# Opening of the first FFN in blocks of 128 channels: scale and shift as single columns on TensorE, squares of x summed there

## The chip, the cores and the metric

The kernel runs on one core of a Trainium2 chip. The metric is device time in microseconds (us), lower is better. The engines of the core are TensorE (PE; PEld is its weight load), VectorE (DVE), ScalarE (ACT), GpSimd (POOL) and SyncE (SP, which issues most of the DMAs).

## The reference, cut to what matters

One encoder layer, 1024 tokens of 1024 channels in f32: an FFN, a mixer of two attentions, and a second FFN, each behind a modulated norm. Scale and shift of every norm come from a conditioning vector through one wide matrix. The change touches only the first norm.

```python
def rms_norm(x, g):
    y = xf * lax.rsqrt(jnp.mean(xf * xf, axis=-1, keepdims=True) + NORM_EPS)
    return (y * g).astype(x.dtype)

def modulate(x, g, shift, scale):
    return rms_norm(x, g) * (1 + scale[:, None, :]) + shift[:, None, :]

cond = jax.nn.silu(c)
mod = (cond @ ada_w[l] + ada_b[l]).reshape(B, N_SUBLAYERS, 3, D_MODEL)
h = modulate(x, norm_g[l, 0], mod[:, 0, 0], mod[:, 0, 1])
x = x + 0.5 * mod[:, 0, 2][:, None, :] * swiglu(h, ffn1_w1[l], ffn1_w3[l], ffn1_w2[l])
```

## The kernel before

Channels lie on the 128 partitions and tokens along the free dimension, so x is eight blocks of 128 channels by two halves of 512 tokens. A scale or a shift of a block is then one column of 128 values. Index i = 0 of the modulation is the shift and i = 1 the scale; each needs the product of `cond` (1024 values, held as eight columns) with a slice of `ada_w`.

A matrix product splits both operands into a rounded f32r part and a rest (`wh`, `wl` and the two tiles named `h`) and takes three f32r matmuls (`mm3`). The first half of the FFN is done in pairs of output blocks (`UpPair`, eleven pairs of fourteen steps) by a scheme with seven products (Strassen's), and the second half in `Down`. A step of a pair is `product`: four channel blocks of three matmuls each, into one PSUM bank. There are eight banks of 512 f32: four tagged "y", for the first products of pairs 0 and 1, and four tagged "b" for everything else. The first two steps of pairs 0 to 3 need only channel blocks 0 to 3 and tokens 0 to 511. They can't start before the norm of these tokens and scale and shift of these blocks are known. That is the opening.

The whole stage up to the end of the first FFN is written down as a list of tasks (class `Plan`) and put in an order by a list scheduler at build time (`flush`, lines 478 to 519): it tries some fifty settings with its own table of durations and keeps the order with the earliest end. Each engine then runs its own queue in that order. Between `nc.inorder = True` and `False` (lines 363 to 386) the DMAs on SP's queue keep the order in which they are written; everything else is free to move as far as data and buffers let it.

The opening as it is written (lines 363 to 395):

- `load_x` brings eight tiles of x, 256 KB each.
- `SquareSum.add` (line 569) squares each tile on ScalarE, and VectorE adds it to a sum `nacc`. Four f32 matmuls of zeros by x warm TensorE up.
- `ModQuarter.load` (line 1546) brings scale and shift weights of 256 channels: per quarter and per index four tiles of 256 KB, whose row pieces are 1 KB. The order on SP's queue is quarter 0, the weights of pairs 0 and 1, quarter 1, those of pairs 2 and 3.
- `norm_rms` sums `nacc` over the partitions by four matmuls with a column of ones, `norm_root` takes the root in twelve small operations of VectorE, and `norm_spread` lays it over all partitions, in one bank.
- For the scale, `ModQuarter.add` (line 1554) accumulates eight weight pieces on VectorE (`macc`) and turns the sum into columns with two matmuls by ones. For the shift, `ModQuarter.row` (line 1565) runs eight matmuls with `cond` as the weight, which give a row of 256 values on one partition (`mrow`), and turns that into columns.
- `mod_done` (line 1594) adds the bias and, for the scale, forms A = (1 + scale) * g.
- `Operands.block` (line 1638) scales the tile of x by A and the root on VectorE, adds the shift on ScalarE while rounding (`h`), and forms the rest on VectorE.
- `run(i)` issues the first two steps of pair i.

Later in the same stage scale and shift of channels 512 to 1023 follow (`ModHalf`), then x blocks 4 to 7 and the other half of the tokens. `t512` takes its tiles from a pool of 52.

Of the kernel before, what the change touches and what calls it, by code (L numbers as in the profile page):

```python
# [11 lines left out]
F32 = mybir.dt.float32  # L12
# [5 lines left out]
AF = mybir.ActivationFunctionType  # L18
ALU = mybir.AluOpType
# [4 lines left out]
D = 1024  # L24
# [3 lines left out]
H = 512  # L28
# [29 lines left out]
class View:  # L58


    def __init__(self, tile, ops):
        self.tile, self.ops = tile, ops
# [500 lines left out]
class SquareSum:  # L563
# [5 lines left out]
    def add(self, x):  # L569
        nc = self.k.nc  # L570
        sq = t512(self.k, name="nsq" if self.acc else "nacc")
        nc.scalar.activation(sq, x, AF.Square)
        if self.acc:
            self.eng.tensor_add(self.acc, self.acc, sq)
        else:
            self.acc = sq
        return sq


def norm_rms(k, acc, tmp, ptile):  # L580

    nc = k.nc
    ps = ptile()
    for b in range(4):
        nc.tensor.matmul(ps[:, b:b + 1], acc[:, b * 128:b * 128 + 128], k.ones_col, start=True, stop=True)
    return norm_root(k, ps[:, 0:4], tmp)


def norm_root(k, t, tmp):

    v = tmp.tile([128, 4], F32, tag="nv", name="nv", bufs=1)
    k.nc.vector.tensor_scalar(v, t, 1.0 / D, EPS, op0=ALU.mult, op1=ALU.add)
    r = tmp.tile([128, 4], F32, tag="nr", name="nr", bufs=1)
    rsqrt(k, r, v, tmp, "na", 1)
    return r
# [132 lines left out]
def t512(k, dt=F32, name="t", home="c"):  # L728

    p, tag, n = k.homes[home]  # L730
    return p.tile([128, H], dt, tag=tag, name=name, bufs=n)
# [748 lines left out]
class ModHalf:  # L1480
# [6 lines left out]
    def load(self, upto):  # L1487
        k = self.k
        for kc in range(len(self.raws), min(8, upto)):
            t = self.tile("mraw")  # L1490
            k.nc.sync.dma_start(t, k.ada_w[kc * 128:kc * 128 + 128, self.i * D + self.h * H:self.i * D + self.h * H + H])
            self.raws.append(t)
# [12 lines left out]
    def columns(self):  # L1505

        t = self.bank()
        for b in range(4):
            self.k.nc.tensor.matmul(t[:, b:b + 1], self.acc[:, b * 128:b * 128 + 128], self.k.ones_col, start=True, stop=True)
        mod_done(self.k, self.i, t, 4 * self.h, 4)  # L1510
# [24 lines left out]
        mod_done(k, self.i, cols, 4 * self.h, 4)  # L1535


class ModQuarter:


    N = 256

    def __init__(self, k, i, q, bank):
        self.k, self.i, self.q, self.bank, self.raws = k, i, q, bank, []

    def load(self, g):
        k, n = self.k, self.N
        t = t512(k, name="mraw")
        c0 = self.i * D + self.q * n
        k.nc.sync.dma_start(t.rearrange("p (a n) -> p a n", a=2),  # L1550
                            k.ada_w[g * 256:g * 256 + 256, c0:c0 + n].rearrange("(a p) n -> p a n", p=128))
        self.raws += [t[:, 0:n], t[:, n:2 * n]]

    def add(self):
        k, nc = self.k, self.k.nc
        acc = t512(k, name="macc")[:, 0:self.N]
        for kc, t in enumerate(self.raws):
            c = k.cond[:, kc:kc + 1]
            if kc == 0:
                nc.vector.tensor_scalar(acc, t, c, None, op0=ALU.mult)  # L1560
            else:
                nc.vector.scalar_tensor_tensor(acc, t, c, acc, op0=ALU.mult, op1=ALU.add)
        self.done(acc, k.ones_col)

    def row(self):
        k, nc = self.k, self.k.nc
        t = self.bank()[0:1, 0:self.N]
        for kc, r in enumerate(self.raws):
            nc.tensor.matmul(t, k.cond[:, kc:kc + 1], r, start=kc == 0, stop=kc == 7)
        r = t512(k, name="mrow")[0:1, 0:self.N]  # L1570
        nc.scalar.activation(r, t, AF.Copy)
        self.done(r, k.ones_col[0:1, :])

    def done(self, v, one):
        t = self.bank()
        for b in range(2):
            self.k.nc.tensor.matmul(t[:, b:b + 1], v[:, b * 128:b * 128 + 128], one, start=True, stop=True)
        mod_done(self.k, self.i, t, 2 * self.q, 2)


def side_by_side(gens):
# [12 lines left out]
def mod_done(k, i, t, b0, n):  # L1594
    nc = k.nc
    m = k.mod[:, i * 8 + b0:i * 8 + b0 + n]
    nc.vector.tensor_add(m, t[:, 0:n], k.ada_b[:, i * 8 + b0:i * 8 + b0 + n])
    s, j = i // 3, i % 3
    c8 = slice(s * 8 + b0, s * 8 + b0 + n)
    if j == 1:  # L1600
        nc.vector.scalar_tensor_tensor(k.A[:, c8], m, 1.0, k.ng[:, c8], op0=ALU.add, op1=ALU.mult)
    elif j == 2:
        nc.vector.tensor_scalar(k.G[:, c8], m, 0.5, None, op0=ALU.mult)
# [619 lines left out]
def layer(tc, xT, c, pos, ada_w, ada_b, ng, inv, w13a, w2a, w_a, w_f, w_q, w_g, fb, fg, dg, wbr, wout, w13b, w2b, out):  # L2223
    with ExitStack() as es:
        k = K()
# [63 lines left out]
        with ExitStack() as ph:  # L2289
            k.wq = wq = Halves(k, pool(w0s, "w0", True, side="right"), 6, [nc.vector, nc.gpsimd])  # L2290
            rp = k.c
# [3 lines left out]
            bank = lambda: pp.tile([128, H], F32, tag="b", name="b", bufs=4)  # L2295
            nc.on = True
            z = t512(k, F32R, "zr")
            nc.gpsimd.memset(z.bitcast(F32), 0.0)
            seed_banks(k, pp, z)
            x = [[t512(k, name="x") for _ in range(2)] for _ in range(8)]  # L2300
            rms = [None, None]
# [5 lines left out]
            pairs = [UpPair(k, i, w13a, wq, bank, d_g[0], nc.vector) for i in range(PAIRS)]  # L2307
# [3 lines left out]
                q.first = True  # L2311
            ops = Operands(k, 0, x, nc.vector)
            mod = {i: ModHalf(k, i, 1, bank) for i in range(2)}
            quarter = [[ModQuarter(k, i, q, bank) for i in range(2)] for q in range(2)]
            k.up_step, k.stores = 0, []

            def consts():
# [46 lines left out]
            for i in range(8):  # L2364
# [2 lines left out]
            nc.gpsimd.memset(on, 1.0)  # L2367
            nc.gpsimd.affine_select(k.ident, on, pattern=[[-1, 128]], compare_op=ALU.is_equal, fill=0.0, base=0,
                                    channel_multiplier=1)
            sq = SquareSum(k, nc.vector)  # L2370
            warm = bank()
            for i in range(8):
                t = sq.add(x[i][0])
                if i < 4:
                    nc.tensor.matmul(warm, z.bitcast(F32)[:, 0:128], x[i][0], start=True, stop=True)
            for n in range(4):
                for m in quarter[0]:
                    m.load(n)
            for i in range(2):
                pairs[i].load1("c", (0,))  # L2380
            for n in range(4):
                for m in quarter[1]:
                    m.load(n)
            for i in range(2, 4):
                pairs[i].load1("c", (0,))
            nc.inorder = False
            rms[0] = norm_rms(k, sq.acc, rp, bank)
            ops.rb[0] = norm_spread(k, rms[0], bank)
            for m in quarter:
                m[1].add()  # L2390
                m[0].row()
            for c in range(4):
                ops.block(c)
            for i in range(4):
                run(i)
# [15 lines left out]
            sq = SquareSum(k, nc.vector)  # L2411
# [63 lines left out]
            ps = [bank() for _ in range(4)]  # L2475
# [100 lines left out]
        bank = lambda: pp.tile([128, H], F32, tag="b", name="b", bufs=4)  # L2576
        with ExitStack() as ph:
# [10 lines left out]
            rp = pool(ph, "rms", True, side="right")  # L2588
# [9 lines left out]
            m = branches(k, w_b, bank, {c: [mods(6)] for c in range(1, 4)})  # L2598
            x = [[t512(k, name="xb") for _ in range(2)] for _ in range(8)]
# [118 lines left out]
```

## Time and profile before

| | us |
|---|---|
| median of 3 runs | 2113.43 |
| lowest and highest run | 2113.41, 2115.27 |
| span of the profiled execution | 2110.5 |

The span runs from the first to the last recorded instruction of the one profiled execution; the page gives no other time of that execution. A run's time is some 3 us longer than the span. A row of the timeline gives start, length, engine, source line, operation, output and inputs by their names in the program, shapes and count; consecutive rows of one kind are merged. All instructions of the planned stage have line L198, that of the scheduler's helper, so they are told apart by tile names. An f32 matmul in the source stands in the trace as two weight loads and two matmuls, an f32r matmul as one of each. Matmuls overlap, so the distance between starts, not the length of one, tells what an instruction costs.

Busy time in the first stretches, in us:

| stretch | PE | DVE | ACT | DMA, GB/s |
|---|---|---|---|---|
| 8 to 10 | 1.79 | 1.69 | 1.87 | 353 |
| 14 to 16 | 1.53 | 1.90 | 0.00 | 359 |
| 18 to 20 | 1.31 | 1.88 | 1.34 | 353 |
| 22 to 24 | 2.00 | 1.97 | 0.00 | 350 |

### The profile page before, as it was taken

The page shows a single profiled execution, that of the slowest core. Times are in us where ns is not written, and L with a number is a line of the kernel's source. Part 1 is how long each engine was busy: PE and PEld are TensorE (multiplying, and loading weights), DVE is VectorE, ACT ScalarE, POOL GpSimd, SP SyncE. Part 2 cuts the span into 40 slices and gives each one's busy share as a digit, 9 for nine tenths or more (in the row PEclk, how much of TensorE's full clock was granted, in tenths as well). Part 3 has the DMA queues.
Part 4 walks back from the last instruction along what each step waited for, and adds up shares of the span by engine and source line. Part 5 has one row for each costly group of instructions (what it writes and reads, how often), then busy time and mean ns, then how long its engine had stood idle before and what let it go on. Part 6 is the DMA issues. An engine that isn't in the chain of part 4 may idle for free.

```text
span 2110.5 us, 30999 instructions
## 1 busy us (share of the span) xinstructions
PE 2094.6 (99%) x10296; PEld 1728.2 (82%) x10296; DVE 1641.7 (78%) x3167; ACT 1135.6 (54%) x2075; POOL 251.1 (12%) x397
## 2 busy tenths in 40 slices
PE   8999999999999999999999999999999999999999
PEld 5887888888888888888888888888888888888887
DVE  7989887869977399886998877979975765568554
ACT  5754444445456266688776776335543333334443
POOL 0022222321100000000444332000000000000000
PEclk9999999999999999999999999999999999999999
DMA  9468888899721555668543224794142523375511
GB/s 347 134 215 275 303 295 274 277 379 366 261 92 48 172 174 192 217 244 274 192 158 99 86 66 160 252 315 154 46 130 100 194 85 129 101 264 206 189 50 41
DMA packets 218285, 398.72 MB, mean 189 GB/s; under 512 B 27198, under 2 KB 69694, under 8 KB 217100
## 3 DMA queue, kind: packets, MB, share of 16 engines
q1 hardware_dynamic: 199772, 339.24, 48.0%
q0 software_dynamic: 18064, 57.46, 7.1%
q8 instruction: 81, 1.33, 0.3%
q14 instruction: 80, 0.66, 0.1%
q10 hardware_dynamic: 288, 0.05, 0.0%
HBM read 282.62 MB, written 114.03 MB: 188 GB/s over the span
## 4 chain that ended last, share of the span: by engine, by line
PE 91%; issue 3%; DVE 2%; DMA 2%; ACT 1%; POOL 1%; SPq 0%; POOLq 0%; DVEq 0%; ACTq 0%
PE b L198 37%; PE y L198 28%; PE pj L198 12%; PE py L198 7%; PE p L198 4%; PE pt L198 4%; DMA mraw<-in_ada_w 0%; POOL d_g L198 0%; DMA f<-d_f 0%; DMA wr<-in_w13b 0%; ACT nt L198 0%; DMA d_wf10l<-pre 0%; DVE z L198 0%; DMA x<-in_xT 0%; ACT h L198 0%
## 5 line engine op out<-in xcount | busy, mean ns | idle before, releaser
L198 PE MATMUL b<-h,wh 128*128 128x512 f32 x1408 | 436.5, 390 | 0.5 <-DVE z L198 0.4
L198 PE MATMUL y<-h,wh 128*128 128x512 f32 x1280 | 397.1, 390 | 0.4 <-ACT h L198 0.3
L198 ACT ACTIVATE wh<-wr 128x512 fp32r<-128x512 f32 x308 | 192.6, 629 | 316.0 <-PE b L198 166.1
L198 PEld LDWEIGHTS b<-h,wh 128*128 128x128 f32 x1408 | 263.2, 188 | 59.1 <-DVE z L198 3.4
L198 PEld LDWEIGHTS y<-h,wh 128*128 128x128 f32 x1280 | 239.6, 188 | 53.4 <-issue 1.2
L198 DVE TENSOR_TENSOR wl<-wr,wh 128x512 fp32r<-128x512 f32 x308 | 208.4, 686 | 94.4 <-ACT wh L198 88.8
L198 PE MATMUL b<-h,wl 128*128 128x512 f32 x704 | 273.6, 389 | 0.0
L198 PE MATMUL y<-h,wl 128*128 128x512 f32 x640 | 249.0, 389 | 0.0
L198 PE MATMUL pj<-wh,h 128*128 128x512 f32 x512 | 161.3, 391 | 0.0
L198 PEld LDWEIGHTS b<-h,wl 128*128 128x128 f32 x704 | 132.2, 188 | 27.7
L198 PEld LDWEIGHTS y<-h,wl 128*128 128x128 f32 x640 | 120.1, 188 | 24.8
L198 ACT ACTIVATE wh<-g 128x512 fp32r<-128x512 f32 x154 | 96.0, 624 | 80.2 <-PE b L198 55.7
L198 PE MATMUL b<-wh 128*128 128x512 f32 x352 | 137.0, 389 | 0.7 <-ACT mrow L198 0.7
L198 DVE TENSOR_TENSOR wl<-a,wh 128x512 fp32r<-128x512 f32 x132 | 90.8, 688 | 59.9 <-ACT wh L198 55.7
L198 PE MATMUL b<-wl,wh 128*128 128x512 f32 x352 | 136.9, 389 | 0.0
L198 PE MATMUL b<-wh,wl 128*128 128x512 f32 x352 | 136.8, 389 | 0.0
L198 ACT ACTIVATE wh<-a 128x512 fp32r<-128x512 f32 x132 | 82.4, 625 | 99.9 <-PE b L198 60.3
L198 DVE TENSOR_TENSOR wl<-g,wh 128x512 fp32r<-128x512 f32 x154 | 105.6, 686 | 29.6 <-ACT wh L198 29.1
L198 POOL TENSOR_SCALAR pr<-pr,mn 128x128 f32<-128x128 f32 (+7 forms) x128 | 102.3, 816 | 167.3 <-DVE mn L198 135.1
L198 ACT ACTIVATE pth<-pt 128x512 fp32r<-128x512 f32 (+1 forms) x160 | 85.5, 554 | 55.9 <-PE pt L198 54.3
L198 DVE TENSOR_TENSOR ptl<-pt,pth 128x512 fp32r<-128x512 f32 (+1 forms) x160 | 97.9, 632 | 20.1 <-ACT pth L198 18.6
L198 PEld LDWEIGHTS pj<-wh,h 128*128 128x128 f32 x512 | 95.7, 188 | 18.6
(382 smaller groups left out, 4376.4 us busy)
## 6 DMA issues: line engine op xcount, KB each, us to landing
g<-d_g SPq DMA_DIRECT2D x154, 256.0 KB, 5.3
mraw<-in_ada_w SPq DMA_DIRECT2D x144, 256.0 KB, 5.7
wr<-in_w13a SPq DMA_DIRECT2D x112, 256.0 KB, 5.4
wr<-in_w13b SPq DMA_DIRECT2D x88, 256.0 KB, 4.8
d_g<-z POOLq DMA_DIRECT2D x77, 256.0 KB, 5.8
d_g<-z SPq DMA_DIRECT2D x77, 256.0 KB, 3.2
a<-in_w2a SPq DMA_DIRECT2D x44, 256.0 KB, 6.3
a<-in_w2b SPq DMA_DIRECT2D x44, 256.0 KB, 5.3
```

The source lines that it names most:

```text
L198: getattr(getattr(self.tc.nc, engine), op)(*map(real, a), **{n: real(v) for n, v in kw.items()})
```

## The change

Scale and shift of the first four channel blocks are no longer made in quarters of 256 channels, but block by block. A block loads its weights as two tiles per index (row pieces of 512 B) and forms its two columns directly: the weight piece is the stationary operand, one column of `cond` the moving one, eight matmuls accumulate a column, the scale's first. VectorE's sums and the shift's rows go. The squares of x stay on ScalarE, but each squared tile is summed over the partitions by four matmuls with the column of ones, and all eight tiles accumulate in four columns of one bank; `nacc` and its additions go. Four matmuls of zeros, which clear that bank, take the place of the warm-up on x. The DMAs on SP's queue are now block 0, pair 0, block 1, pairs 1 and 2, block 2, pair 3, block 3. The columns of a block are written down ahead of that block's operands.

```diff
@@ -1535,47 +1535,33 @@
         mod_done(k, self.i, cols, 4 * self.h, 4)
 
 
-class ModQuarter:
-
-
-    N = 256
-
-    def __init__(self, k, i, q, bank):
-        self.k, self.i, self.q, self.bank, self.raws = k, i, q, bank, []
-
-    def load(self, g):
-        k, n = self.k, self.N
-        t = t512(k, name="mraw")
-        c0 = self.i * D + self.q * n
-        k.nc.sync.dma_start(t.rearrange("p (a n) -> p a n", a=2),
-                            k.ada_w[g * 256:g * 256 + 256, c0:c0 + n].rearrange("(a p) n -> p a n", p=128))
-        self.raws += [t[:, 0:n], t[:, n:2 * n]]
-
-    def add(self):
-        k, nc = self.k, self.k.nc
-        acc = t512(k, name="macc")[:, 0:self.N]
-        for kc, t in enumerate(self.raws):
-            c = k.cond[:, kc:kc + 1]
-            if kc == 0:
-                nc.vector.tensor_scalar(acc, t, c, None, op0=ALU.mult)
-            else:
-                nc.vector.scalar_tensor_tensor(acc, t, c, acc, op0=ALU.mult, op1=ALU.add)
-        self.done(acc, k.ones_col)
-
-    def row(self):
-        k, nc = self.k, self.k.nc
-        t = self.bank()[0:1, 0:self.N]
-        for kc, r in enumerate(self.raws):
-            nc.tensor.matmul(t, k.cond[:, kc:kc + 1], r, start=kc == 0, stop=kc == 7)
-        r = t512(k, name="mrow")[0:1, 0:self.N]
-        nc.scalar.activation(r, t, AF.Copy)
-        self.done(r, k.ones_col[0:1, :])
-
-    def done(self, v, one):
+class ModBlock:
+
+
+    def __init__(self, k, c, bank):
+        self.k, self.c, self.bank = k, c, bank
+
+    def load(self):
+
+        k, c = self.k, self.c
+        self.raws = {}
+        for i in (1, 0):
+            for j in range(2):
+                t = t512(k, name="mraw")
+                c0 = i * D + c * 128
+                k.nc.sync.dma_start(t.rearrange("p (a n) -> p a n", a=4),
+                                    k.ada_w[j * H:j * H + H, c0:c0 + 128].rearrange("(a p) n -> p a n", p=128))
+                self.raws[i, j] = t
+
+    def columns(self):
+
+        k, nc, c = self.k, self.k.nc, self.c
         t = self.bank()
-        for b in range(2):
-            self.k.nc.tensor.matmul(t[:, b:b + 1], v[:, b * 128:b * 128 + 128], one, start=True, stop=True)
-        mod_done(self.k, self.i, t, 2 * self.q, 2)
+        for i in (1, 0):
+            for kc in range(8):
+                w = self.raws[i, kc // 4][:, kc % 4 * 128:kc % 4 * 128 + 128]
+                nc.tensor.matmul(t[:, i:i + 1], w, k.cond[:, kc:kc + 1], start=kc == 0, stop=kc == 7)
+            mod_done(k, i, t[:, i:i + 1], c, 1)
 
 
 def side_by_side(gens):
@@ -2311,7 +2297,7 @@
                 q.first = True
             ops = Operands(k, 0, x, nc.vector)
             mod = {i: ModHalf(k, i, 1, bank) for i in range(2)}
-            quarter = [[ModQuarter(k, i, q, bank) for i in range(2)] for q in range(2)]
+            blocks = [ModBlock(k, c, bank) for c in range(4)]
             k.up_step, k.stores = 0, []
 
             def consts():
@@ -2367,29 +2353,24 @@
             nc.gpsimd.memset(on, 1.0)
             nc.gpsimd.affine_select(k.ident, on, pattern=[[-1, 128]], compare_op=ALU.is_equal, fill=0.0, base=0,
                                     channel_multiplier=1)
-            sq = SquareSum(k, nc.vector)
-            warm = bank()
+            ps = bank()
+            for _ in range(4):
+                nc.tensor.matmul(ps, z[:, 0:128], z, start=True, stop=True)
             for i in range(8):
-                t = sq.add(x[i][0])
-                if i < 4:
-                    nc.tensor.matmul(warm, z.bitcast(F32)[:, 0:128], x[i][0], start=True, stop=True)
-            for n in range(4):
-                for m in quarter[0]:
-                    m.load(n)
-            for i in range(2):
-                pairs[i].load1("c", (0,))
-            for n in range(4):
-                for m in quarter[1]:
-                    m.load(n)
-            for i in range(2, 4):
-                pairs[i].load1("c", (0,))
+                t = t512(k, name="nsq")
+                nc.scalar.activation(t, x[i][0], AF.Square)
+                for b in range(4):
+                    nc.tensor.matmul(ps[:, b:b + 1], t[:, b * 128:b * 128 + 128], k.ones_col, start=False, stop=i == 7,
+                                     skip_group_check=True)
+            for c in range(4):
+                blocks[c].load()
+                for i in ((0,), (1, 2), (3,), ())[c]:
+                    pairs[i].load1("c", (0,))
             nc.inorder = False
-            rms[0] = norm_rms(k, sq.acc, rp, bank)
+            rms[0] = norm_root(k, ps[:, 0:4], rp)
             ops.rb[0] = norm_spread(k, rms[0], bank)
-            for m in quarter:
-                m[1].add()
-                m[0].row()
             for c in range(4):
+                blocks[c].columns()
                 ops.block(c)
             for i in range(4):
                 run(i)
```

## The prediction

> **What bounds the kernel now.** I read the page first, for the bounding engine.
>
> ```profile
> span 2110.5 us, 30999 instructions
> PE 2094.6 (99%) x10296; PEld 1728.2 (82%) x10296; DVE 1641.7 (78%) x3167; ACT 1135.6 (54%) x2075; POOL 251.1 (12%) x397
> ```
>
> TensorE is busy for 99% of the span. A saved instruction on another engine is worth something only where TensorE waits for it. So the second view is the chain of waits at the start (start, length, what), which is the stage that changes.
>
> ```profile
> 4.09 5.21 DMA x<-in_xT
> 9.32 6.03 DMA mraw<-in_ada_w
> ...
> 19.34 0.76 DVE x L198
> 20.12 0.73 ACT h L198
> 20.89 0.73 PE y L198 x2
> 21.63 0.95 PE b L198 x4
> 22.58 1.36 PE y L198 x5
> 23.94 0.95 PE b L198 x4
> 24.89 1.35 PE y L198 x5
> 26.24 0.95 PE b L198 x4
> 27.20 0.89 PE y L198 x3
> 28.09 0.53 PE b L198 x4
> 28.62 0.66 PE y L198 x2
> 29.28 0.34 PE b L198 x4
> 29.62 1.74 PE y L198 x7
> ...
> 387.25 5.44 PE y L198 x24
> ```
>
> Up to 20.89 the first product waits for x (landed at 9.30), the scale and shift weights (15.35), and then a serial tail of TensorE and VectorE. From 20.89 on every row is TensorE. The "y" rows are the first products; the "b" rows between them are the scale and shift of channels 256 to 511, with 3 x 0.95 + 0.53 + 0.34 = 3.7 us. The last row gives the price of a product instruction in a steady stream: 5.44 / 24 = 0.227 us. The third view, TensorE's waits from 30 to 720 us, asks whether anything later can still be won.
>
> ```profile
> PE b L198 <- ACT mrow L198: 0.7, 1, 0.7
> PE b L198 <- DVE z L198: 0.4, 1, 0.4
> ```
>
> Two more are 0.2 each, 1.5 us in all. After 20.89 the opening is bound by the number of TensorE instructions. So I compare one number: **the time of the first product plus all TensorE work behind it that isn't a product**. Before, that is 20.9 + 3.7 = 24.6 us (work common to both kernels, from 33 us on, left out).
>
> **The change part by part.**
>
> ```profile
> 47.53 1.84 PE L198 MATMUL b<-ones_col,macc 128*128 128x1 f32 x16
> 49.23 0.72 PE L198 MATMUL b<-h,wh 128*128 128x512 f32 x2
> ...
> 62.56 1.05 PE L198 MATMUL b<-ident,nr 128*128 128x128 f32 x8
> 63.37 0.71 PE L198 MATMUL y<-h,wh 128*128 128x512 f32 x2
> ```
>
> *Price of a single column.* Eight source matmuls of a full-width weight by one column stand as 16 instructions, so each f32 matmul is two. They start at 47.53, and the next product starts at 49.23: 1.70 / 16 = 0.106 us an instruction. The spread of the root-mean-square is 8 instructions in 63.37 - 62.56 = 0.81 us.
>
> *Removed.* Two quarters of the shift as rows (16 instructions of 0.95 / 4 = 0.24 us each), their turn into columns, the four matmuls that end the sum of squares, four f32 warm-up matmuls on x, and on VectorE the sums below.
>
> ```profile
> L198 DVE SCALAR_TENSOR_TENSOR macc<-mraw,cond,macc 128x256 f32<-128x256 f32 x14 | 6.7, 482 | 0.2
> L198 DVE TENSOR_TENSOR nacc<-nacc,nsq 128x512 f32<-128x512 f32 x7 | 4.8, 692 | 4.9 <-ACT nsq L198 4.4
> ```
>
> VectorE sheds 6.7 + 4.8 us and two 0.35 us starts. Four more additions and two more products on the modulation columns come to it, about 1 us by the 0.15 of the nv row below. From 30 us on TensorE waited 0.4 us for VectorE in all, so of that relief only what lies ahead of the first product counts.
>
> *Squares on TensorE.* Eight tiles x 4 matmuls x 2 = 64 instructions, 6.8 us at 0.106, 0.85 us a tile.
>
> ```profile
> 4.49 0.63 ACT L198 ACTIVATE nacc<-x 128x512 f32<-128x512 f32 x1 [1.26 <-DMA x<-in_xT]
> ...
> 6.66 4.04 ACT L198 ACTIVATE nsq<-x 128x512 f32<-128x512 f32 x6 [0.90 <-DMA x<-in_xT]
> ```
>
> ScalarE delivers the first squares at 5.1, the third at 7.3, and from there one every 0.67 us to 10.70. TensorE needs 0.85 for each, so it falls behind from the third on: 7.3 + 6 x 0.85 = 12.4 us. That holds at full clock. The clock was not full from the start:
>
> ```profile
> 7.23 0.34 PEld L198 LDWEIGHTS b<-x,zr 128*128 128x128 f32 x1 [0.52 <-issue]
> 7.91 0.19 PEld L198 LDWEIGHTS b<-x,zr 128*128 128x128 f32 x1 [0.34 <-issue]
> ```
>
> A weight load took 0.34 until 7.23 and 0.19 from 7.91. That is 0.15 more, which makes a slow single column about 0.26, an estimate from these two rows. If the clock rises at 7.5 again, nine instructions are done by then and 55 x 0.106 = 5.8 follow: 13.3 us. The squares end at **12.4 to 13.3**.
>
> *The root.* Twelve VectorE operations, for the second half at 59.58 to 61.91 (two rows, first and last):
>
> ```profile
> 59.58 0.15 DVE L198 TENSOR_SCALAR nv<-b 128x4 f32<-128x4 f32 x1
> 61.74 0.17 DVE L198 SCALAR_TENSOR_TENSOR nr<-na,nr 128x4 f32<-128x4 f32 x1
> ```
>
> These are 2.3 us on a free VectorE, so the root is there at 14.7 to 15.6. TensorE meanwhile does block 0.
>
> *Columns.* Each block is 2 x 8 x 2 = 32 instructions, 3.4 us: 13.6 us for four blocks, where rows and their turns took 3.8 + 0.5 + 0.3 a quarter, 9.3 in all. Block 0 follows the squares (12.4 to 15.8, or 13.3 to 16.7), and with the spread of 0.8 TensorE reaches 16.6 or 17.5. Scaling and h then take the 0.76 + 0.73 of the chain, and the first product starts at 18.1 to 19.0, some 2.4 us sooner than now. Meanwhile TensorE runs block 1's columns.
>
> *DMA.* The bytes and their place on SP's queue are nearly the same: 16 tiles of modulation weights and 8 of products, now as 4, 2, 4, 4, 4, 2, 4 instead of 8, 4, 8, 4; what SP issues behind them keeps its order. A row piece shrinks from 1 KB to 512 B. The nearest rows are windows 10 to 16 us (1 KB) and 88.4 to 94 us (two tiles of 512 B pieces; 40 slices each):
>
> ```profile
> DMA packets 2106, 2.17 MB, mean 361 GB/s; under 512 B 130, under 2 KB 1968, under 8 KB 2106
> GB/s 132 219 103 161 263 190 44 29 88 205 219 179 73 139 146 179 274 315 348 329 333 344 344 344 340 307 260 241 172 410 435 391 388 322 88 59 0 0 0 0
> DMA packets 1359, 1.18 MB, mean 210 GB/s; under 512 B 80, under 2 KB 1104, under 8 KB 1359
> ```
>
> In its full stretch (340 or so) a 256 KB tile takes 0.77 us, by the mean of 210 it takes 1.25; I take 0.77, as the queue is full here. Block 3 lands at 9.3 + 16 x 0.77 + 8 x 0.73 = 27.5 and its h is there some 2.8 us later, at 30.3 (0.85 for its last tile's columns, 0.4 for the small sums by the 0.15 of the nv row and their turns, then scaling and h). TensorE has 10.2 us of columns and 12.2 of products (three pairs, three blocks, 18 x 0.68) from 16.6 on, enough until 39. So DMA is hidden. At 1.25 a tile h comes at 38, still hidden; the cover is gone near 1.3.
>
> *Waits added.* TensorE's queue now holds squares that wait for ScalarE, with nothing urgent behind them. Both columns of a block share a bank, so TensorE may wait for VectorE's read of the first: nothing, or 4 x 0.25 us. I take nothing, as they are different columns, and keep 1.0 for the range. A switch from columns to products costs: the six y rows, 24 products, last 6.73 us where 24 x 0.227 is 5.44, so 0.2 a switch. Blocks 1 to 3 make three to twelve switches against six: -0.6 to +1.2, taken as 0.
>
> **The sum.** Squares to 12.4 (13.3), block 0 3.4, spread 0.8, blocks 1 to 3 10.2: 26.8 to 27.7 us, against 24.6. That is +2.2 to +3.1; I take +2.6. The products begin sooner, but TensorE has more to do between them, and from there on it is the bound.
>
> *The rest of the stage.* The order up to 668 us is planned anew.
>
> ```profile
> 668.25 2.31 PE L198 MATMUL b<-wa,h 128*128 128x432 f32 x11
> ```
>
> The stage holds 2772 products (11 pairs x 168, and 7 x 11 x 12), 628.4 us. With 24.6 of opening, 1.7 of late columns, two norms of 1.7 and 16 row matmuls of 0.23 that makes 662; 6 us are lost in small gaps. Another plan may lose 4 to 9: -2 to +3 us, an estimate.
>
> **Rivals.** *1. Single columns are cheaper.* The 1.70 us behind the price of 0.106 may hold one switch of 0.2; without it 1.50 / 16 is 0.094. The 64 + 32 + 96 instructions then take 192 x 0.012 = 2.3 us less: +0.3, 2113.7. For it: the y rows show such switches. Against it: a weight load of 128 columns stands behind each instruction, and the spread's eight, with 128 columns each, took 0.101. *2. Slower: the clock stays low under the squares.* A single-column matmul streams one column per weight load, and the four zero matmuls end about 4.8 us in. If this stream doesn't raise the clock, 64 instructions at 0.26 from 5.1 end at 21.7 instead of 12.4: +9.3, with the 2.2 makes +11.5, so 2124.9. It passes +4.2 when the clock is still low at about 9.3 us (16 slow instructions, each 0.15 late, less the 0.4 that TensorE would wait for the third square). For it: the clock rose only at 7.5, some 3 us into dense full-width matmuls. Against it: the 16 instructions of 47.53 were narrow too and the products behind them kept their pace, though that is only 1.7 us. [...] *3. A luckier plan* wins back over 6 us of gaps: under 2109.2; all 6 us would have to go.
>
> **How the numbers follow.** The span is 2110.5 and the runs' median 2113.4; the 2.9 us outside the span stay. 2110.5 + 2.9 + 2.6 = **2116.0 us**. Chances: forecast 0.60, rival 1 0.24, rival 2 0.13, rival 3 0.03. What a measurement can tell from no change is 0.2%, 4.2 us. The forecast's spread (-2 to +3 of the plan, +1 of the bank) puts a quarter of it, 0.15, above 2117.7, and a sliver of rival 1, 0.01; with rival 2 that is 0.29 slower. Faster is rival 3 and 0.01 of rival 1, together 0.04; 0.67 remains. The range, 2111.5 to 2121.5, takes in the plan and the bank on both, and leaves out rival 3 and most of rival 2.
>
> **What would show it.** Right: first y product at 18 to 19 us; 64 instructions on nsq ending near 13 us; blocks of 32 column instructions at 0.106; TensorE unbroken from there; some 2 to 3 us later at the same product. Wrong: slow weight loads past 9 us (rival 2), TensorE waiting for mraw tiles or for mod between blocks, or a count of gaps to 668 us that differs by more than the opening does.

## The result: slower, 2113.42 to 2140.93 us

| | before | after |
|---|---|---|
| median of four runs, us | 2113.42 | 2140.93 |
| lowest and highest run, us | 2111.43, 2115.27 | 2139.09, 2143.80 |
| span of the profiled execution, us | 2110.5 | 2139.1 |
| products recorded in the first 100 us | 311 | 196 |
| last product with `wa`, the next weights, starts at, us | 707.5 | 736.3 |

The ratio is 1.0132, with an interval of 1.0120 to 1.0144: **27.5 us slower**, where +2.6 was forecast and the range ended at +8.1. The loss is complete by the end of the planned stage: the last product with `wa` is 28.8 us late and the whole span 28.6.

The head of the page of the changed kernel (span, busy time, busy tenths):

```profile
span 2139.1 us, 31263 instructions
...
PE 2123.6 (99%) x10428; PEld 1765.8 (83%) x10428; DVE 1632.7 (76%) x3150; ACT 1134.6 (53%) x2073; POOL 249.8 (12%) x397
...
PEclk5999999999999999999999999999999999999999
```

TensorE is as busy as before, 99%. What is new is one digit: the granted clock of the first slice (53 us) is 5. The page of before has 9 there:

```profile
PEclk9999999999999999999999999999999999999999
```

TensorE's windows of the changed kernel show where (stretch, its length, busy time and instructions of PE, granted clock, DMA share, GB/s):

```profile
4.00:8.00 4.00, 3.41 (x22) 1.00 0.98 317
8.00:12.00 4.00, 4.00 (x24) 0.60 1.11 326
...
48.00:56.00 8.00, 7.75 (x26) 0.50 0.70 225
56.00:60.00 4.00, 4.00 (x18) 0.93 0.17 55
```

In the stretches between, the mean is 0.50 throughout, so the clock is read here as either full or half. Then a mean of 0.60 over 8 to 12 us is 0.8 us at full clock and 3.2 at half, and 0.93 over 56 to 60 is 0.56 at half: the clock **fell to half at 8.8 us and came back at 56.6**. TensorE is busy in every one of these stretches. It isn't idle, it is slow. Its timeline in the changed kernel (start, length, instruction, count, idle time before):

```profile
5.34 1.96 PE L198 MATMUL b<-ones_col,nsq 128*128 128x1 f32 x16 [0.18 <-ACT nsq L198]
7.71 9.43 PE L198 MATMUL b<-ones_col,nsq 128*128 128x1 f32 x48 [0.41 <-ACT nsq L198]
17.00 5.26 PE L198 MATMUL b<-cond,mraw 128*128 128x1 f32 x24
...
33.18 1.20 PE L198 MATMUL y<-h,wh 128*128 128x512 f32 x2
...
48.49 2.72 PE L198 MATMUL b<-cond,mraw 128*128 128x1 f32 x12 [0.25 <-DVE mod L198]
51.07 1.20 PE L198 MATMUL y<-h,wh 128*128 128x512 f32 x2
...
57.15 0.40 PE L198 MATMUL y<-h,wl 128*128 128x512 f32 x1
```

Squares end at 17.0, the first product starts at 33.2 (forecast 18.1 to 19.0), and products run without columns between them from 51.1. Twelve column instructions from 48.49 to 51.07 cost 0.215 us each, twice the 0.106 of the forecast. The products cost nearly twice as much too: fifteen from 51.07 to 57.15, the last of them after the clock's return, are 0.405 each, against 0.227. The chain of waits of the changed kernel agrees; it is TensorE alone, with four short stops at VectorE:

```profile
7.71 14.56 PE b L198 x72
...
22.30 0.17 DVE mod L198
```

### The profile page after: what moved, and what is told of

Read it like the earlier page. It is cut to its first block, busy times and chain, and to the rows that moved or that the text cites. A ratio compares the mean times of both kernels' runs of the same rounds, so it can differ in the third digit from the quotient of the medians.

```text
span 2139.1 us, 31263 instructions
## 1 busy us (share of the span) xinstructions
PE 2123.6 (99%) x10428; PEld 1765.8 (83%) x10428; DVE 1632.7 (76%) x3150; ACT 1134.6 (53%) x2073; POOL 249.8 (12%) x397
## 3 DMA queue, kind: packets, MB, share of 16 engines
q1 hardware_dynamic: 203868, 339.24, 47.8%
## 4 chain that ended last, share of the span: by engine, by line
PE 91%; DVE 2%; issue 2%; ACT 2%; DMA 2%; POOL 0%; SPq 0%; ACTq 0%; DVEq 0%; POOLq 0%
PE b L198 38%; PE y L198 28%; PE pj L198 12%; PE py L198 7%; PE p L198 4%; PE pt L198 4%; ACT nt L198 1%; DVE wl L198 0%; ACT wh L198 0%; DMA g<-d_g 0%; DMA d_wq2l<-pre 0%; DVE z L198 0%; DMA f<-d_f 0%; ACT h L198 0%; DVE macc L198 0%
## 5 line engine op out<-in xcount | busy, mean ns | idle before, releaser
L198 PEld LDWEIGHTS b<-h,wl 128*128 128x128 f32 x704 | 132.2, 188 | 27.7
```

The source lines that it names most:

```text
L198: getattr(getattr(self.tc.nc, engine), op)(*map(real, a), **{n: real(v) for n, v in kw.items()})
```

## The experiments

Two questions were open. Is it the single columns that bring the clock down, or something that the change takes away (the warm-up matmuls on x)? And what would the change cost at full clock? The expectations call the rival explanations theories A to C; the first one says what they are.

For all of them one more number is used, read from the groups of TensorE instructions in the first 100 us: the products recorded there. 100 us less 0.2267 us for each is the time that went into anything else, the index of the prediction with the later work left in. It is 29.5 for the kernel before (311 products) and 55.6 for the changed one (196), 26.1 apart.

### The squares alone

The kernel before, with the squares summed on TensorE as in the change; quarters and rows stay.

```diff
-            sq = SquareSum(k, nc.vector)
-            warm = bank()
+            ps = bank()
+            for _ in range(4):
+                nc.tensor.matmul(ps, z[:, 0:128], z, start=True, stop=True)
...
-            rms[0] = norm_rms(k, sq.acc, rp, bank)
+            rms[0] = norm_root(k, ps[:, 0:4], rp)
```

> The kernel before with only the squares moved to TensorE (and the four zero matmuls instead of the warm-up on x); scale and shift stay in quarters. Theory A (a stream of single columns counts as idle, so the clock falls some 3.6 us after it starts and comes back only after about 5 us of dense matmuls): clock at half from about 9 us, squares end at 17 us, the 256-column rows behind them are dense and raise it again near 22 to 24 us; about +4 us, 2117.5. Theory B (the warm-up on x was what held the clock, and it is gone here): the clock stays at half until the products have run for 5 us, some +7 us, 2120. Theory C (the columns' place in the order costs the time, the clock is a side effect): no columns here, so within 2 us of the kernel before.

Measured: 2120.34, ratio 1.0036 (1.0023 to 1.0050), 7.4 us slower. The windows of this kernel:

```profile
8.00:10.00 2.00, 2.00 (x14) 0.64 1.02 367
...
22.00:24.00 2.00, 1.54 (x8) 0.94 1.10 347
```

The clock falls at 8.6 (0.64 over two us) and is back at 22.2. It fell under the 64 single columns, which start at 5.44, and came back under the rows behind them, 256 columns wide, which start at 17.39. That is the course of rival 2, low under the squares and back behind them; but 7.4 is not 27.5. The time alone is nearer to theory B (2120) than to A (2117.5). The clock decides against B, which has it at half from the start: the squares instructions start 0.11 us apart, the price at full clock, from 5.44 until the fall.

### The columns alone

The changed kernel, with squares, sum and warm-up on x as before (the same lines as above, the other way round).

> The changed kernel with the squares back on VectorE and the warm-up on x back; scale and shift still as single columns by block. Theory A: the clock is full at 7.5 us, the stream of columns starts near 10 us, the clock falls near 13.5 us and comes back some 5 us after the last column; 96 of 128 instructions at 0.21 instead of 0.106: about +14 us, 2127. Theory B: the clock stays full and the opening ends about 1 us later than before: 2114.5. Theory C: most of the loss is here, +20 us or more, whatever the clock does.

Measured: 2135.56, ratio 1.0106 (1.0076 to 1.0135), 22.6 us slower. So the warm-up on x doesn't cure it. The number is also what theory C expected (20 us or more); the wide and the turned kernel below, which keep the blocks and the order of the DMAs, decide against that. Windows of this kernel:

```profile
10.00:12.00 2.00, 0.67 (x2) 1.00 1.17 319
12.00:16.00 4.00, 1.47 (x8) 0.61 1.15 323
...
48.00:52.00 4.00, 4.00 (x14) 0.70 1.05 382
```

Here the clock falls at 12.9, before the columns begin (18.2): after the warm-up TensorE has little to do (0.67 of the 2 us from 10 to 12). It then stays at half through all 128 column instructions and is back at 50.4, when products have run since 47.05. That is why the time lies above what was expected of single columns alone: all of them ran at half. The two parts don't add up, 7.4 and 22.6 against 27.5, since they share one stretch of low clock.

### Dense matmuls among the narrow ones

The changed kernel with added matmuls of zeros, 508 or 510 columns wide, which accumulate nothing into unused columns: one for eight narrow instructions (this diff), or one for four (every second in place of every fourth).

```diff
+                    if b % 4 == 3:
+                        nc.tensor.matmul(ps[:, 4:], z[:, 0:128], z[:, 4:], start=False, stop=i == 7, skip_group_check=True)
...
+                if kc % 4 == 3:
+                    nc.tensor.matmul(t[:, 2:], z[:, 0:128], z[:, 2:], start=False, stop=kc == 7, skip_group_check=True)
```

> The changed kernel with one dense matmul of zeros (508 or 510 columns, into unused columns of the same bank) after every 8 instructions of squares and of columns, and one that clears each block's bank: about a fifth of the stream is dense. The output is the same. Theory A: if a fifth is enough to count as busy, the clock stays full and the 28 added matmuls cost 6.4 us: 26.8 + 6.4 + 1 for the waits on the shared bank against 24.6, about +9.5 us, 2123. If it is not enough, the added matmuls run at half clock and the time is 2150. Theories B and C: nothing is gained, 2141 plus 6 to 12 us.

> The same with a dense matmul after every 4 instructions: about a third of the stream is dense. Theory A: the clock stays full, 52 added matmuls cost 11.8 us: about +15 us, 2128.5; with too little density 2161. Theories B and C: 2141 plus 12 to 24 us.

Measured: 2170.34 (ratio 1.0270, 1.0229 to 1.0312) and 2180.84 (1.0320, 1.0287 to 1.0353), above everything that was expected. The planner put the added matmuls of the squares ahead of all squares, since nothing ties them to one another, so that part wasn't tried. The timeline of the denser kernel:

```profile
7.95 9.21 PE L198 MATMUL b<-ones_col,nsq 128*128 128x1 f32 x64
...
20.33 0.85 PE L198 MATMUL b<-cond,mraw 128*128 128x1 f32 x4
21.04 0.77 PE L198 MATMUL b<-zr 128*128 128x510 f32 x1
21.61 0.85 PE L198 MATMUL b<-cond,mraw 128*128 128x1 f32 x4
```

Among the columns they do stand where they were meant to, one for four: 0.43 us of dense work (the price of a product at half clock) in each 1.28, from 20.33 to 21.61. That third didn't raise the clock, which was down: it is granted 0.50 from 20 to 28 us. The index of the two is 60.1 and 70.1, so 30.6 and 40.6 of the 57.4 and 67.9 us lie in the opening. The rest came later in the stage: from 60 to 760 us TensorE waits 9.0 us for `wh` of ScalarE in the first of the two, and not at all in the kernel before. Why `wh` is late there was not tested.

### Streams of known density

To see the clock by itself, the kernel before got six streams of added work, on constants, in its steady part (results unused): single columns (a), single columns with one dense matmul for eight, four, two (b, c, d), and the turned form, the column as weight and 128 or 256 columns streaming (e, f).

```diff
+            def stream(part, n):
+                t = bank()
+                nc.tensor.matmul(t, z[:, 0:128], z, start=True, stop=False, skip_group_check=True)
+                forms = {"c": (t[:, 0:1], k.ident, k.ones_col), "d": (t[:, 4:], z[:, 0:128], z[:, 4:]),
+                         "r": (t[0:1, 0:128], k.ones_col, k.ident), "q": (t[0:1, 0:256], k.ones_col, z.bitcast(F32)[:, 0:256])}
+                calls = [("matmul", forms[f], dict(start=False, stop=False, skip_group_check=True)) for f in part * n]
+                nc.together(10.2, *calls)
```

> The kernel before with six streams of idle work on TensorE, each about 10 us at full clock and one task that nothing else can enter, set into the steady part some 45 us apart: a 96 single-column instructions; b the same with a dense 508-column matmul after every 8; c after every 4; d after every 2; e 48 f32 matmuls of a one-column weight by 128 columns; f 22 of a one-column weight by 256 columns. Theory A (single columns count as idle, whatever came before): in a the granted clock falls to half 3.4 to 6.8 us after its start and comes back some 3.4 to 7 us into the products behind it; e and f, whose instructions stream 128 or 256 columns, keep it full; b to d show the share of dense work that is enough. Rival (the opening never raised the clock firmly; a warm TensorE keeps it): all six run at full clock and take 10 us each, 61 us in all.

Measured: one run, 2213.47; only its trace matters. Stream a starts at 113.54, b at 184.97, c at 240.98, d at 295.9, e at 344.67, f at 394.3. Windows of this kernel:

```profile
114.00:118.00 4.00, 4.00 (x38) 1.00 0.62 191
118.00:120.00 2.00, 2.00 (x16) 0.75 0.28 110
...
132.00:134.00 2.00, 2.00 (x9) 0.84 0.00 0
...
190.00:192.00 2.00, 2.00 (x13) 0.67 0.68 250
...
203.00:206.00 3.00, 3.00 (x12) 0.78 0.01 5
...
245.00:246.00 1.00, 1.00 (x6) 0.64 1.04 402
...
258.00:260.00 2.00, 2.00 (x8) 0.77 0.00 0
297.00:307.00 10.00, 10.00 (x66) 1.00 0.64 211
345.00:355.00 10.00, 10.00 (x94) 1.00 0.77 261
```

By these means, read as above, the falls are at 119.00 (0.75 over two us), 190.68 and 245.28, and the returns at 132.64, 204.32 and 258.92. Streams d, e and f hold full clock (f has 1.00 from 394 to 404). Three things follow. First, 38 single columns in 4 us: at full clock the price of 0.106 was right. Second, **the clock fell in a, b and c and held in d, e and f**. By the price of a product, an estimate, b has about 20% of dense time (0.227 in 1.12 us a group), c has 34% (0.227 in 0.67), and d has half (22 groups in 10 us, 0.227 in 0.45). Third, the clock didn't follow at once. The falls came 5.46, 5.71 and 4.30 us after the streams' starts, and each return 13.64 after its fall, 3.73, 3.19 and 2.63 into the products behind the streams. For a, 5.46 and 3.73 are within what was expected. What sets these times was not shown.

In the changed kernel no gap on TensorE between 5.34 us and the return is over 0.41 us, and the clock fell.

### The same products at full clock

The changed kernel with one edit: the moving column is repeated to 128 columns, so each instruction streams as many columns as its weight has. The results are those of the column, 128 times.

```diff
-                    nc.tensor.matmul(ps[:, b:b + 1], t[:, b * 128:b * 128 + 128], k.ones_col, start=False, stop=i == 7,
+                    nc.tensor.matmul(ps[:, b * 128:b * 128 + 128], t[:, b * 128:b * 128 + 128],
+                                     k.ones_col.to_broadcast([128, 128]), start=False, stop=i == 7, ...
...
-                nc.tensor.matmul(t[:, i:i + 1], w, k.cond[:, kc:kc + 1], start=kc == 0, stop=kc == 7)
+                nc.tensor.matmul(t[:, i * 128:i * 128 + 128], w, k.cond[:, kc:kc + 1].to_broadcast([128, 128]), ...
```

> The changed kernel, nothing moved and nothing added: only the moving operand of the squares and of the modulation columns is the same column repeated 128 times, so that each instruction streams 128 columns, which fits into the time of its weight load (0.10 to 0.12 us, as the spread's instructions show); every column of a block's result is the same, one is used. Theory A: the clock never falls, and what is left is the forecast's own sum of TensorE instructions, +2.6 (and 1 us of waits on the shared bank): 2114 to 2119. If it stays above 2130, the width of the stream is not what decides.

Measured: 2120.85 against 2113.86, ratio 1.0031 (1.0020 to 1.0043), 7.0 us slower, 2 us above the 2114 to 2119 that were expected. The granted clock is 1.00 in every window of the opening; the one that has 0.60 in the changed kernel reads

```profile
8.00:12.00 4.00, 4.00 (x38) 1.00 1.10 333
```

In these 4 us TensorE gets through 38 instructions instead of 24. With 128 times the columns to stream, the same instructions are done **20 us sooner** (2140.93 - 2120.85). The timeline of TensorE in this kernel:

```profile
5.50 7.52 PE L198 MATMUL b<-ones_col,nsq 128*128 128x128 f32 x64 [0.34 <-ACT nsq L198]
12.86 2.84 PE L198 MATMUL b<-cond,mraw 128*128 128x128 f32 x24
...
16.28 1.05 PE L198 MATMUL b<-ident,nr 128*128 128x128 f32 x8
17.17 3.29 PE L198 MATMUL b<-cond,mraw 128*128 128x128 f32 x28
20.71 1.38 PE L198 MATMUL b<-cond,mraw 128*128 128x128 f32 x10 [0.25 <-DVE mod L198]
21.85 0.72 PE L198 MATMUL y<-h,wh 128*128 128x512 f32 x2
...
22.64 0.39 PE L198 MATMUL y<-h,wh 128*128 128x512 f32 x1
24.17 2.69 PE L198 MATMUL b<-cond,mraw 128*128 128x128 f32 x22 [1.14 <-DMA mraw<-in_ada_w]
...
31.90 1.60 PE L198 MATMUL b<-cond,mraw 128*128 128x128 f32 x12 [0.25 <-DVE mod L198]
33.26 0.71 PE L198 MATMUL y<-h,wh 128*128 128x512 f32 x2
```

This is the forecast's kernel, and its terms can be read off; the section on the prediction does so.

### Where a column becomes wide enough

The streams again, all of one form, 96 instructions each with 128 weight columns, and 16, 32, 48, 64, 96 or 128 columns streaming.

> The kernel before with six streams of 96 instructions (48 f32 matmuls of a 128-column weight) in the steady part, one task each, whose moving operand is 16, 32, 48, 64, 96 and 128 columns wide. [...] Theory A with the bound between a third (fell) and a half (held) of the streams before: the clock falls in the first three, holds in the last two, and 64 is the edge. If only the weight loads or the number of instructions counted, all six would behave alike.

Measured: one run, 2219.60. The groups of the six streams (count, busy time, mean ns):

```profile
L198 PE MATMUL b<-ones_col,ident 128*128 128x16 f32 x96 | 17.9, 343 | 0.0
L198 PE MATMUL b<-ones_col,ident 128*128 128x32 f32 x96 | 17.6, 361 | 0.0
L198 PE MATMUL b<-ones_col,ident 128*128 128x48 f32 x96 | 16.8, 359 | 0.0
...
L198 PE MATMUL b<-ones_col,ident 128*128 128x128 f32 x96 | 10.9, 273 | 0.0
...
L198 PE MATMUL b<-ones_col,ident 128*128 128x64 f32 x96 | 10.8, 274 | 0.0
```

The window around the stream of 48 columns shows the low clock; the streams of 16 and 32 have 0.50 too (116 to 128 and 192 to 204 us), those of 64, 96 and 128 columns have 1.00 (301 to 312, 350 to 361 and 399 to 410):

```profile
242.00:262.00 20.00, 20.00 (x110) 0.65 0.80 268
```

At 48 columns the clock fell, at 64 it held, and 64 to 128 columns cost the same (10.8 to 10.9 us). How much of an instruction's time a width streams stands in no row. The 256 columns of stream f took 9.7 us for 44 instructions, 0.22 each, and the 128 of stream e 10.6 for 96, 0.11 each. From that 48 and 64 columns are estimated at 38% and 50% of the 0.11; stream c, with 34%, fell and d, with half, held. Weight loads alone didn't hold the clock: each stream has 96 loads of 128 columns, and the clock fell in three of the six.

### Turned: rows in place of columns

The changed kernel, with the one-column operand as the weight and the data streaming, and the row turned back into a column, as the kernel before does with its shift.

```diff
-                for b in range(4):
-                    nc.tensor.matmul(ps[:, b:b + 1], t[:, b * 128:b * 128 + 128], k.ones_col, start=False, stop=i == 7, ...
+                nc.tensor.matmul(ps[0:1, :], k.ones_col, t, start=i == 0, stop=i == 7)
...
-                nc.tensor.matmul(t[:, i:i + 1], w, k.cond[:, kc:kc + 1], start=kc == 0, stop=kc == 7)
+                nc.tensor.matmul(t, k.cond[:, kc:kc + 1], w, start=kc == 0, stop=kc == 7)
```

> The changed kernel with every single-column product turned round: the column of ones or of cond is the weight, and the tile of squares (512 columns) or the weight piece (128 columns) streams; the rows that come out are copied by ScalarE and turned into columns by one small matmul each. Order, DMAs and number of accumulating matmuls per block are those of the changed kernel, the array time of the streams is about the same. Theory A: the clock stays full and the loss goes; with the copies and turns about +5 us, 2118. Theory C (blocks, order and waits cost the time): within 6 us of the changed kernel, 2135 to 2147.

Measured: 2121.82, ratio 1.0043 (1.0027 to 1.0059), 8.3 us slower (about 5 was expected), with the clock at 1.00 throughout. Another way out of the low clock, at 1 us more than repeating the column; the way back from rows to columns delays the first product to 23.7.

### The new order with the old operations

The changed kernel's blocks and DMA order, with sums on VectorE and rows as before.

```diff
+        for kc, w in enumerate(raws[1]):
...
+                nc.vector.scalar_tensor_tensor(acc, w, s, acc, op0=ALU.mult, op1=ALU.add)
...
+        for kc, w in enumerate(raws[0]):
+            nc.tensor.matmul(t, k.cond[:, kc:kc + 1], w, start=kc == 0, stop=kc == 7)
```

> DMAs and order by block of 128 channels as in the change, but the operations of before: squares added on VectorE with the warm-up on x, scale on VectorE, shift as rows. Theory A: the clock stays full, the first products start 2 to 3 us sooner than before and half of what TensorE does for the blocks lies ahead of them: -2 to +1 us, 2112. Theory C: +10 us or more, 2123.

Measured: 2117.86, ratio 1.0026 (1.0015 to 1.0037), 4.3 us slower, where theory A expected -2 to +1 at full clock. In the windows of this kernel the clock is low again, now where TensorE has little to do (0.61 of the 2 us from 10 to 12):

```profile
12.00:16.00 4.00, 1.55 (x8) 0.58 1.14 323
16.00:20.00 4.00, 3.65 (x20) 0.57 1.13 335
```

So the new order by itself wins nothing. How much of the 4.3 is the clock and how much VectorE's sums (TensorE waits 1.5 us for `macc`) was not separated.

### The squares alone, wide

The kernel before with squares on TensorE, the column of ones repeated to 128.

> The kernel before with only the squares on TensorE, streamed 128 columns wide. Theory A: no fall of the clock; squares end near 13 us as with VectorE, the root is there 1 us sooner because VectorE doesn't share its time with the sums of squares: -2 to +1 us, 2111 to 2114.5; the single-column form took about 7 us more than the kernel before.

Measured: 2114.03 against 2113.86, ratio 1.0003 (0.9994 to 1.0013): the same. Without the low clock the squares cost nothing and win nothing. The chain of waits of this kernel says why:

```profile
5.36 11.13 PE b L198 x80
...
20.95 0.74 PE y L198 x2
```

Squares and then the shift's rows keep TensorE in one piece until 16.49. In the kernel before it had waited for the last weights (landed at 15.35) and made the rows of these, to 16.43. Work stands where a wait stood, and the first product starts at 20.95 instead of 20.89. The root is there 0.3 us sooner (16.25 instead of 16.57), not 1.

### Two banks for the two columns

The wide kernel, with scale and shift of a block in a bank each, so that TensorE need not wait while VectorE reads the first.

```diff
-        t = self.bank()
         for i in (1, 0):
+            t = self.bank()
```

> The wide form with a bank of its own for each of a block's two columns, so that TensorE needn't wait for VectorE's read of the scale before it goes on with the shift. If the four waits of 0.25 us are part of the 7 us that the wide form still loses, they vanish and the time is 1 us lower, near 2120; if the waits only stand in front of a later wait for DMA, nothing is gained: 2121.

Measured: 2120.90, ratio 1.0037 (1.0024 to 1.0049), the same as the wide kernel's 2120.85. TensorE's waits up to 720 us, of the kernel with two banks:

```profile
PE b L198 <- DMA mraw<-in_ada_w: 1.5, 1, 1.5
...
PE b L198 <- DVE nr L198: 1.1, 1, 1.1
```

The wide kernel had 1.1 at the DMA and 1.0 in four waits for `mod`. The four are gone; TensorE waits longer for block 2's weights instead, and 1.1 for the root. A wait removed ahead of another is not won.

### The runs side by side

| kernel | measured against before, us | products in 100 us | index against before, us |
|---|---|---|---|
| the change | +27.5 | 196 | +26.1 |
| columns alone | +22.6 | 210 | +22.9 |
| turned | +8.3 | 277 | +7.7 |
| squares alone | +7.4 | 281 | +6.8 |
| wide | +7.0 | 286 | +5.7 |
| wide, two banks | +7.2 | 283 | +6.3 |
| new order, old operations | +4.3 | 287 | +5.4 |
| squares alone, wide | +0.2 | 311 | 0.0 |

The last column is 0.2267 times the products missing against 311. The two dense kernels (+57.4 and +67.9), which lose time later too, and the two with streams are left out. In each of these kernels the whole difference, to 1.4 us, is made in the first 100 us. No version beats the kernel before.

## Why the prediction was wrong

**The step that failed** is the price of a single column. It was right where it was read and wrong where it was used. The row at 47.53 covers 1.7 us, between stretches of products. The forecast used it for 192 instructions, 20 us at that price; in the changed kernel the clock fell 3.5 us after the first of them (5.34 to 8.8). From 8.8 us on their price is 0.215, and the spread and the products near them, which the sum has at full clock, cost about double too. The same row was named as the evidence against rival 2 ("products behind them kept their pace"), with the remark that it is only 1.7 us; that remark was the point.

**Rival 2** had the cause, not its extent. It let the clock stay low under the squares and come back behind them, +9.3. In the changed kernel the clock was up when the squares began (0.11 us an instruction at 5.34), fell at 8.8, 3.5 us later, and did not come back under the spread's 128 columns (from 22.96 to 24.81), the single columns and two groups of four products (from 33.18 and 42.13). The price, from the changed kernel against the wide one: squares end 17.00 instead of 12.86, 4.1; 128 columns x (0.215 - 0.113) = 13.1; the spread 1.85 instead of 0.89, 1.0; products at half clock, two groups of four 1.85 instead of 1.02 and fifteen 6.08 instead of 3.4, 4.3. Less the DMA wait of 1.3 that the slow columns hide, that is 21.2; measured 20.1. Its estimate of 0.26 for a slow column was too high: half clock makes 0.215.

**The clock before the squares.** "The clock rises at 7.5 again" took the kernel before as the pattern. The changed kernel runs eight zero matmuls ahead of the squares. The last of these start 0.43 us apart, about twice the 0.227 of a product, and the squares from 5.34 on 0.11: that the clock came up in between is an estimate from these prices, and the windows give 1.00 from the start. They do so in the kernel before too, where the forecast read the rise from the weight loads. That was in the forecast's favour, and worth nothing 3.5 us later.

**What held, by the wide kernel.** The squares end at 12.86 (12.4 to 13.3), the spread takes 0.89 (0.8), and h of block 0 is there when it was said to be: its ScalarE row in the wide kernel's timeline ends at 18.96 (18.1 to 19.0). The first product itself starts only at 21.85: it stands behind the rest of block 1's columns in TensorE's queue. The sum counts TensorE's work and not its order, so this costs nothing in it, but the first sign of being right fails even at full clock.

```profile
18.24 0.72 ACT L198 ACTIVATE h<-x,mod 128x512 fp32r<-128x512 f32 x1 [1.79 <-DVE mod L198]
```

**What was mis-sized, by the same kernel.** From its timeline above: the products run unbroken from 33.26, with eight before, so 33.26 - 8 x 0.227 = 31.4 us of opening, where the sum had 26.8 to 27.7. The 4.2 over its middle:

- *Bank waits, 1.7 instead of 0.* "I take nothing, as they are different columns" is refuted: 28 columns of 0.111 from 17.17 end at 20.28, the next starts at 20.71, and that stands four times, 0.43 each (the waits list 0.25 of each).
- *DMA, 1.3 instead of 0.* "DMA is hidden" failed on the order and on the time of landing. "Enough until 39" counted all columns and products as free to fill in, but the plan put block 2's columns behind only four products. These end at 22.9, and TensorE then waited 1.14 us for the weights of block 2 and did nothing else. By the forecast's prices the first tile of block 2, the ninth of the modulation and behind six of the products, would still have been in time: 9.3 + 9 x 0.77 + 6 x 0.73 = 20.6. It landed at 24.03, as the row of the wide kernel's chain below says, and the columns start at 24.17. What makes it land 3.4 us late was not separated.
- *Column price, 0.111 instead of 0.106*, read at the spread (0.89 / 8): 128 times, 0.6.
- The remaining 0.6 lies in starts and changes between kinds.

```profile
17.12 6.91 DMA mraw<-in_ada_w
```

With these the forecast's +2.6 would be +6.8; the wide kernel measured +7.0, and its 2120.85 is still within the range of 2111.5 to 2121.5. So without the low clock the direction of the forecast is right and its size low: TensorE gets more to do, and it is the bound.

**Rivals 1 and 3.** Single columns weren't cheaper at full clock (38 in 4 us is 0.105, in the squares 0.11), and no plan won back more than it lost.

## What to carry to other kernels

A matmul that streams one column for a full weight load cost 0.106 us here in a stretch of 1.7 us and 0.215 once the clock had fallen, 3.2 us (squares alone) to 5.5 us (stream a) after the first of them. Where such matmuls run for longer than that, read the granted clock: TensorE was 99% busy here, and at half clock for 47.8 us (8.8 to 56.6). Repeating the moving column to 64 columns or more cost next to nothing here and kept the clock (96 instructions in 10.8 us with 64 columns, 17.9 with 16); turning the operands kept it too, at 1 us more in all. And a price read from a short stretch holds for a longer one only if the granted clock stays what it was.

## What was not expected of the hardware

- A weight load for each matmul didn't keep the clock: with 16, 32 and 48 f32 columns per 128 weight columns it fell to 0.50, with 64 it held at 1.00.
- The return came some us into wide work. In the changed kernel products run without columns between them from 51.07, and the clock is back 5.5 us later; with the columns alone it took 3.4 (from 47.05), in the streams 2.6 to 3.7. With the squares alone it came 4.8 us after the rows began (17.39), and with the old operations 3.1 us after the spread began (16.35). What makes it 2.6 in one and 5.5 in another was not separated.
- At half clock the weight load slows too: in the changed kernel a load of the squares takes 192 ns from 5 to 8 us and 333 ns from 9 to 16. Single columns, whose weight loads follow without a break (PEld is busy for 8.00 of the 8 us from 8 to 16), went from 0.106 to 0.215 us.
- The clock also fell behind a stretch with little work: with 0.67 us of TensorE work between 10 and 12 us it fell at 12.9 in the kernel with the columns alone, and under the columns it stayed down, for 37.5 us in all. In the kernel with the old operations, which has a similar stretch and rows behind it, it was down for 6.8 us (12.64 to 19.44).
